# Rows transposed, split and multiplied in two halves of 256 tokens at two of the norms ahead of a projection, and the first loads in another order

## Chip, cores and metric

One core of one Trainium2 chip runs the whole kernel. The metric is the device time of one execution in microseconds (us), the median of three runs. TensorE (PE) multiplies and transposes, VectorE (DVE), ScalarE (ACT) and GpSimd (POOL) work on tiles, and SyncE (SP) issues most of the loads. Each engine works through its own row of instructions, and semaphores hold an instruction back until what it reads is there.

## What is computed

Two transformer blocks over 512 tokens of 1024 channels, in float32. Six times rows are normed and then projected; the change is at the first and the last of the six.

```python
def rms_norm(x, g, eps=NORM_EPS):
    x32 = x.astype(jnp.float32)
    y = x32 * lax.rsqrt(jnp.mean(x32 * x32, axis=-1, keepdims=True) + eps)
    return (y * g.astype(jnp.float32)).astype(x.dtype)

def first_block(x, norm_mix_pre_g, w_in, ...):
    h = rms_norm(x, norm_mix_pre_g[l])
    proj = h @ w_in[l]                       # the first place
    ...
def second_block(x, mem, ...):
    x = x + 0.5 * swiglu(rmsnorm(x, ffn1_norm[l]), ffn1_w_gu[l], ffn1_w_down[l])
    ...
    x = x + memory_cross_attention(rmsnorm(x, mem_q_norm[l]), ..., mem_w_o[l])
    x = x + 0.5 * swiglu(rmsnorm(x, ffn2_norm[l]), ffn2_w_gu[l], ffn2_w_down[l])   # the last place
    return rmsnorm(x, final_norm)
```

## The kernel before

Tokens lie in four tiles of 128 (t), channels in eight tiles of 128 (k). A float32 product is made of three: each operand is split into a high and a low half (`split`, lines 399 to 406: ScalarE writes the high half, VectorE subtracts it from the source for the low half), and high x high, high x low and low x high are added up in a PSUM bank. Weights come in slabs of 1024 rows by 256 columns, a `wr` tile that two DMAs of 512 KB fill; each of its two parts of 128x1024 elements is halved into `wh` and `wl` (lines 402 and 403).

`PreNorm.operand` (line 475) turns normed rows into the right operand of the next projection and multiplies the first slab at once. Its steps, with the names of the trace:

- `scale` (lines 469 to 474): per token tile, two instructions on ScalarE and VectorE scale the rows by their reciprocal root, into `y` tiles of 128x512. At the first place the sums of squares go ahead of it (lines 454 and 563), then a sum (447) and a power on GpSimd (448).
- `flip` (line 489): TensorE transposes, 32 in all. One PSUM bank `b` per k holds 512 tokens. The first six k (`AHEAD`) are transposed token tile by token tile, the last two between the products.
- `split` with the gain (lines 405 and 406): bank k becomes two tiles `h` of 128x512, high and low.
- products (line 513): for each k six of 128x512 columns into the two banks `a`.

TensorE's row is in the order of the program text here (`manual_schedule`). The rows of the other engines are set by a scheduler that goes by priorities: loads and halvings of weights have a high one (`WPRIO`), the splits of the norm too (`SPRIO`), and `in_order` ties the first three splits and one halving of weights (`LATER`, `PINS`) into one order. `later` holds the second halving of the first slab. The next slab is halved among the splits.

`x_rows` (line 188) issues the eight loads of x, each 256 KB. The first place stands at line 569, the last at line 1771, where `wide` (line 1103), the projection ahead of it, multiplies token tile by token tile and its `emit` adds (line 1677), squares and scales each finished tile.

Of the kernel before, what the change touches and what calls it, by code (L numbers as in the profile page):

```python
# [18 lines left out]
P = 128  # L19
# [74 lines left out]
def transformer_blocks_kernel(  # L94
# [55 lines left out]
    def big(tag, bufs, dt=F32, cols=512):  # L150
        return sp.tile([P, cols], dt, tag=tag, bufs=bufs, name=nm(tag))
# [13 lines left out]
    def acc():  # L165
        return pa.tile([P, 512], F32, tag="a", name=nm("a"))

    def aux():
        return pb.tile([P, 512], F32, tag="b", name=nm("b"))
# [15 lines left out]
    junk = cp.tile([P, 512], F32, name="junk")  # L185
    junk2 = sp.tile([P, 512], F32, tag="w", bufs=WBUFS, name="junk2")

    def x_rows(src, get=None):

        res = {}  # L190
        for t in range(4):
            for u in range(2):
                tl = (get or wt)()
                tc.keep_in_program_order(
                    nc.sync.dma_start(tl, src[t * P:(t + 1) * P, u * 512:(u + 1) * 512]))
                res[t, u] = tl
        return res

    with tc.high_priority(2 * WPRIO):
        vec0 = wt()[:8, :P]  # L200
        nc.sync.dma_start(vec0, norm_mix_pre_g.rearrange("a (k p) -> (a k) p", p=P))
        xt = x_rows(x[0])
        gps = aux()
        T.transpose(gps[:, :8], vec0, ident[:8, :8])
        gain0 = cp.tile([P, 8], F32, name="gain0")
        V.tensor_copy(gain0, gps[:, :8])
# [54 lines left out]
    def wload(raw, src, k, n, cols):  # L261
        with tc.high_priority(WPRIO):
            nc.sync.dma_start(raw[:, :n * cols].rearrange("p (k c) -> p k c", c=cols),
                              src[k * P:(k + n) * P, :].rearrange("(k p) c -> p k c", p=P))

    def wslab(src, kt, cols, later=None):
        return list(wpieces(src, kt, cols, later))

    def wpieces(src, kt, cols, later=None):

        per = max(1, 1024 // cols)
        for k in range(0, kt, per):
            n = min(per, kt - k)
            if k % (2 * per) == 0:
                whole = raw_slab()
            raw = whole[:, k % (2 * per) * cols:][:, :n * cols]
            wload(raw, src, k, n, cols)
            hi, lo = [t[:, :n * cols] for t in halves_w()]
            halve = lambda hi=hi, lo=lo, raw=raw: split(hi, lo, raw)
            if later is None or k == 0:  # L280
                with tc.high_priority(WPRIO):
                    halve()
            else:
                later.append(halve)
            yield k, n, hi.rearrange("p (k c) -> p k c", c=cols), lo.rearrange("p (k c) -> p k c", c=cols)
# [128 lines left out]
    @contextmanager  # L414
    def in_order(chain):

        traced = nc.cur_bb.bb.instructions
        last = traced[-1]
        yield
        start = next(k for k in reversed(range(len(traced))) if traced[k] is last) + 1  # L420
        for i in traced[start:]:
            if i.engine in QUEUES:
                if i.engine in chain:
                    tc.add_manual_dep(i, chain[i.engine], mybir.DependencyInfo(
                        mybir.DependencyClass.NoSync, mybir.DependencyReason.DATA))
                chain[i.engine] = i.name
# [30 lines left out]
    class PreNorm:  # L457
# [18 lines left out]
        def operand(self, src, *before):  # L476
# [36 lines left out]
                            T.matmul(accs[m], lh, rh, start=c == 0 and n in (0, 2), stop=c == KT - 1 and n > 3)  # L513
            return res, accs

    class PostNorm:


# [47 lines left out]
                if t:  # L566
                    pre.scale(t - 1, [xt[t - 1, 0], xt[t - 1, 1]], rs[t - 1], act=t < 4)
    with tc.issue_after(pows[-1].ins):
        h, ready = pre.operand(w_in[0][:, :256])

# [1195 lines left out]
        weave(chains, fills, WIDTH3, BANKS3, MODEL3)  # L1768
    pre, emit = residual("ffn2")
    wide(mem_w_o_2[0], KT, mo, emit, WIDE_K, True, begun, HELD)  # L1770
    h, ready = pre.operand(ffn2_w_gu_2[0][:, :256])


    fg = []
# [54 lines left out]
```

## Time and profile before

| | us |
|---|---|
| median of 3 runs (1914.20 to 1915.53) | 1914.49 |
| profiled execution | 1915.45 |
| its span | 1913.7 |
| PE busy (98% of the span) | 1881.5 |
| DVE busy (72%) | 1387.2 |
| ACT busy (49%) | 929.2 |
| POOL busy (9%) | 175.0 |

The share of the chain that ended last is 88% PE. Mean traffic is 101 GB/s, the DMA queue that carries nearly all of it is busy for 29.8% of 16 engines' span. Busy shares are means over stages with different limits, so a place is read by the rows of its own stretch: start and duration in us, then the engine, the line and the tiles (output <- inputs), and in brackets how long the engine had sat idle before and what ended that. "x3" merges three instructions in a row.

### The profile page before, as it was taken

How to read it: one execution, taken by the hardware profiler on the slowest of the kernel's cores; microseconds unless marked ns; L12 is line 12 of the kernel's file. 1: busy time of each engine (PE TensorE's matmuls, PEld its weight loads, DVE VectorE, ACT ScalarE, POOL GpSimd, SP SyncE). 2: the span in 40 equal slices, each digit the busy share in tenths (PEclk: the TensorE clock that was granted, in tenths of full speed). 3: DMA queues.
4: the chain of work that ended last, by engine and by line, in shares of the span. 5: the costliest groups of instructions: out<-in, count | busy, mean ns of one | idle time of the engine just before them, and what ended most of it. 6: DMA issues, size and time to landing. Idle time of an engine off the chain costs nothing.

```text
span 1913.7 us, 29312 instructions
## 1 busy us (share of the span) xinstructions
PE 1881.5 (98%) x11566; PEld 1688.7 (88%) x11566; DVE 1387.2 (72%) x2217; ACT 929.2 (49%) x1537; POOL 175.0 (9%) x272
## 2 busy tenths in 40 slices
PE   8999999999999999999999999999999999999998
PEld 7899888888999998889999988888978778999997
DVE  6777635468878786677878757888866448878785
ACT  5666534364544344444344456668555344344443
POOL 2240100050000002000000010330510000000000
PEclk9999999999999999999999999999989999999999
DMA  5221223462232324423232343211223222332322
GB/s 180 67 67 56 78 66 133 143 203 89 89 111 89 114 97 168 151 89 102 97 111 88 111 148 101 67 45 45 89 89 110 77 81 82 102 111 89 111 89 89
DMA packets 161452, 192.40 MB, mean 101 GB/s; under 512 B 7361, under 2 KB 131362, under 8 KB 161314
## 3 DMA queue, kind: packets, MB, share of 16 engines
q1 hardware_dynamic: 159746, 185.80, 29.8%
q0 software_dynamic: 1280, 4.20, 0.6%
q8 instruction: 91, 1.49, 0.3%
q10 hardware_dynamic: 288, 0.52, 0.1%
q14 instruction: 47, 0.39, 0.1%
HBM read 182.11 MB, written 8.39 MB: 100 GB/s over the span
## 4 chain that ended last, share of the span: by engine, by line
PE 88%; issue 5%; DVE 3%; ACT 2%; POOL 2%; POOLq 0%; ACTq 0%; DVEq 0%
PE b L372 16%; PE b L373 16%; PE b L371 16%; PE a L371 11%; PE a L372 11%; PE a L373 11%; PE a L513 4%; PE b L615 1%; PE b L1444 1%; PE b L489 1%; DVE wl L403 1%; PE b L753 1%; DVE w L1540 0%; ACT wh L402 0%; PE b L883 0%
## 5 line engine op out<-in xcount | busy, mean ns | idle before, releaser
L403 DVE TENSOR_TENSOR wl<-wr,wh 128x1024 fp32r<-128x1024 f32 (+1 forms) x381 | 463.5, 1220 | 269.9 <-ACT wh L402 266.1
L402 ACT CAST wh<-wr 128x1024 fp32r<-128x1024 f32 (+1 forms) x381 | 394.0, 1036 | 443.0 <-PE b L372 154.5
L371 PE MATMUL b<-wh,q 128*128 128x512 f32 x672 | 262.4, 390 | 0.0
L372 PE MATMUL b<-wl,q 128*128 128x512 f32 x672 | 262.0, 390 | 0.0
L373 PE MATMUL b<-wh,q 128*128 128x512 f32 x664 | 257.9, 389 | 0.0
L371 PE MATMUL a<-h,wh 128*128 128x512 f32 (+1 forms) x660 | 238.4, 361 | 0.0
L373 PE MATMUL a<-h,wl 128*128 128x512 f32 (+1 forms) x660 | 234.9, 356 | 0.0
L372 PE MATMUL a<-h,wh 128*128 128x512 f32 (+1 forms) x660 | 234.7, 356 | 0.0
L372 PE MATMUL b<-h,wh 128*128 128x256 f32 (+1 forms) x568 | 175.9, 310 | 0.0
L371 PE MATMUL b<-h,wh 128*128 128x256 f32 (+1 forms) x568 | 175.9, 310 | 0.0
L373 PE MATMUL b<-h,wl 128*128 128x256 f32 (+1 forms) x568 | 175.9, 310 | 0.0
L371 PEld LDWEIGHTS b<-wh,q 128*128 128x128 f32 x672 | 126.3, 188 | 24.7
L373 PEld LDWEIGHTS b<-wh,q 128*128 128x128 f32 x664 | 124.6, 188 | 26.5
L372 PEld LDWEIGHTS b<-wl,q 128*128 128x128 f32 x672 | 126.3, 188 | 24.3
L372 PE MATMUL a<-s,wh 128*128 128x256 f32 (+1 forms) x488 | 141.2, 289 | 0.0
L373 PEld LDWEIGHTS a<-h,wl 128*128 128x128 f32 x660 | 124.5, 189 | 18.3
L371 PEld LDWEIGHTS a<-h,wh 128*128 128x128 f32 x660 | 124.7, 189 | 17.9 <-issue 0.5
L372 PEld LDWEIGHTS a<-h,wh 128*128 128x128 f32 x660 | 124.8, 189 | 17.8 <-issue 0.5
L372 PEld LDWEIGHTS b<-h,wh 128*128 128x128 f32 x568 | 108.3, 191 | 5.6
L373 PEld LDWEIGHTS b<-h,wl 128*128 128x128 f32 x568 | 108.2, 191 | 5.6
L371 PEld LDWEIGHTS b<-h,wh 128*128 128x128 f32 x568 | 108.1, 190 | 5.6
L372 PEld LDWEIGHTS a<-s,wh 128*128 128x128 f32 x488 | 93.1, 191 | 1.3
(374 smaller groups left out, 4195.9 us busy)
## 6 DMA issues: line engine op xcount, KB each, us to landing
wr<-in_ffn_w_gu_dram SPq DMA_DIRECT2D x88, 512.0 KB
wr<-in_w_in_dram SPq DMA_DIRECT2D x68, 512.0 KB
wr<-in_ffn_w_down_dram SPq DMA_DIRECT2D x44, 512.0 KB
wr<-in_w_gate_dram SPq DMA_DIRECT2D x22, 512.0 KB
wr<-in_w_up_dram SPq DMA_DIRECT2D x22, 512.0 KB
wr<-in_w_down_dram SPq DMA_DIRECT2D x22, 512.0 KB
wr<-in_mem_w_kv_dram SPq DMA_DIRECT2D x16, 512.0 KB
wr<-in_w_out_dram SPq DMA_DIRECT2D x10, 512.0 KB
```

Source lines behind the costliest of these rows:

```text
L371: T.matmul(ps, lh, rh, start=first, stop=False)
L372: T.matmul(ps, lh, rl, start=False, stop=False)
L373: T.matmul(ps, ll, rh, start=False, stop=last)
L402: A.copy(hi, src)
L403: V.tensor_tensor(lo, src, f32(hi), op=ALU.subtract)
L489: T.transpose(banks[k][:, t * P:(t + 1) * P], self.s[t, k // 4][:, (k % 4) * P:(k % 4 + 1) * P], ident)
L513: T.matmul(accs[m], lh, rh, start=c == 0 and n in (0, 2), stop=c == KT - 1 and n > 3)
L615: T.matmul(ps, lh[n], rh[n], start=n == 0, stop=n == 1)
L753: T.transpose(ps[:, o * P:(o + 1) * P], blk, ident)
L1444: T.matmul(ps[:, gg * 64:(gg + 1) * 64], e[:, gg * P:(gg + 1) * P], up, start=True, stop=True)
```

## The change

A second method, `operand_by_halves`, is used at the first and at the last norm. A bank now holds two k of 256 tokens. The transposes of tokens 0 to 255 come first, then their splits (128x256) and products (128x256 columns) for six k, then the transposes of tokens 256 to 511, the other two k, and the splits and products of the second half. At the first place the loads go in the order x of tokens 0 to 255, first part of the first weight slab, x of the rest, second part; `wslab` takes that slab as `loaded`.

```diff
@@ -185,10 +185,10 @@
     junk = cp.tile([P, 512], F32, name="junk")
     junk2 = sp.tile([P, 512], F32, tag="w", bufs=WBUFS, name="junk2")
 
-    def x_rows(src, get=None):
+    def x_rows(src, get=None, tokens=range(4)):
 
         res = {}
-        for t in range(4):
+        for t in tokens:
             for u in range(2):
                 tl = (get or wt)()
                 tc.keep_in_program_order(
@@ -199,7 +199,14 @@
     with tc.high_priority(2 * WPRIO):
         vec0 = wt()[:8, :P]
         nc.sync.dma_start(vec0, norm_mix_pre_g.rearrange("a (k p) -> (a k) p", p=P))
-        xt = x_rows(x[0])
+        xt = x_rows(x[0], tokens=range(2))
+        raw0 = sp.tile([P, 2048], F32, tag="wr", bufs=2, name="wr0")
+        for k in (0, 4):
+            tc.keep_in_program_order(
+                nc.sync.dma_start(raw0[:, k * 256:(k + 4) * 256].rearrange("p (k c) -> p k c", c=256),
+                                  w_in[0][k * P:(k + 4) * P, :256].rearrange("(k p) c -> p k c", p=P)))
+            if k == 0:
+                xt.update(x_rows(x[0], tokens=range(2, 4)))
         gps = aux()
         T.transpose(gps[:, :8], vec0, ident[:8, :8])
         gain0 = cp.tile([P, 8], F32, name="gain0")
@@ -263,18 +270,21 @@
             nc.sync.dma_start(raw[:, :n * cols].rearrange("p (k c) -> p k c", c=cols),
                               src[k * P:(k + n) * P, :].rearrange("(k p) c -> p k c", p=P))
 
-    def wslab(src, kt, cols, later=None):
-        return list(wpieces(src, kt, cols, later))
-
-    def wpieces(src, kt, cols, later=None):
+    def wslab(src, kt, cols, later=None, loaded=None):
+        return list(wpieces(src, kt, cols, later, loaded))
+
+    def wpieces(src, kt, cols, later=None, loaded=None):
 
         per = max(1, 1024 // cols)
         for k in range(0, kt, per):
             n = min(per, kt - k)
-            if k % (2 * per) == 0:
+            if loaded is not None:
+                whole = loaded
+            elif k % (2 * per) == 0:
                 whole = raw_slab()
             raw = whole[:, k % (2 * per) * cols:][:, :n * cols]
-            wload(raw, src, k, n, cols)
+            if loaded is None:
+                wload(raw, src, k, n, cols)
             hi, lo = [t[:, :n * cols] for t in halves_w()]
             halve = lambda hi=hi, lo=lo, raw=raw: split(hi, lo, raw)
             if later is None or k == 0:
@@ -513,6 +523,51 @@
                             T.matmul(accs[m], lh, rh, start=c == 0 and n in (0, 2), stop=c == KT - 1 and n > 3)
             return res, accs
 
+        def operand_by_halves(self, src, loaded=None):
+
+            with tc.manual_schedule(engines={mybir.EngineType.PE}):
+                later, chain = [], {}
+                slab = {k + j: (hi[:, j, :], lo[:, j, :]) for (k, n, hi, lo) in wslab(src, KT, 256, later, loaded)
+                        for j in range(n)}
+                accs = [acc() for m in range(2)]
+                res = [(big("h", 16, F32R), big("h", 16, F32R)) for k in range(KT)]
+
+                def flips(half):
+
+                    banks = [aux() for k in range(0, KT, 2)]
+                    for t in range(2):
+                        for k in range(KT):
+                            o = k % 2 * 256 + t * P
+                            T.transpose(banks[k // 2][:, o:o + P],
+                                        self.s[2 * half + t, k // 4][:, (k % 4) * P:(k % 4 + 1) * P], ident)
+                    return banks
+
+                def operands(half, banks):
+                    sl = slice(half * 256, half * 256 + 256)
+                    for k in range(KT):
+                        with tc.high_priority(SPRIO), in_order(chain) if half == 0 and k <= PINS else nullcontext():
+                            split(*[t[:, sl] for t in res[k]], banks[k // 2][:, k % 2 * 256:k % 2 * 256 + 256],
+                                  gcol(self.g, k))
+                            if half == 0 and k == LATER:
+                                later[0]()
+
+                def products(half, ks):
+                    sl = slice(half * 256, half * 256 + 256)
+                    for c in ks:
+                        hh, hl = [t[:, sl] for t in res[c]]
+                        terms = [(slab[c][part][:, m * P:(m + 1) * P], hh, m) for m in range(2) for part in range(2)]
+                        terms += [(slab[c][0][:, m * P:(m + 1) * P], hl, m) for m in range(2)]
+                        for n, (lh, rh, m) in enumerate(terms):
+                            T.matmul(accs[m][:, sl], lh, rh, start=c == 0 and n in (0, 2), stop=c == KT - 1 and n > 3)
+
+                operands(0, flips(0))
+                products(0, range(AHEAD))
+                banks = flips(1)
+                products(0, range(AHEAD, KT))
+                operands(1, banks)
+                products(1, range(KT))
+            return res, accs
+
     class PostNorm:
 
 
@@ -566,7 +621,7 @@
                 if t:
                     pre.scale(t - 1, [xt[t - 1, 0], xt[t - 1, 1]], rs[t - 1], act=t < 4)
     with tc.issue_after(pows[-1].ins):
-        h, ready = pre.operand(w_in[0][:, :256])
+        h, ready = pre.operand_by_halves(w_in[0][:, :256], raw0)
 
 
 
@@ -1768,7 +1823,7 @@
         weave(chains, fills, WIDTH3, BANKS3, MODEL3)
     pre, emit = residual("ffn2")
     wide(mem_w_o_2[0], KT, mo, emit, WIDE_K, True, begun, HELD)
-    h, ready = pre.operand(ffn2_w_gu_2[0][:, :256])
+    h, ready = pre.operand_by_halves(ffn2_w_gu_2[0][:, :256])
 
 
     fg = []
```

ScalarE at the first place, from the load of its table on. In the rows `w` are x tiles (w_82 and w_86 of token tiles 0 and 1), `y` scaled rows, `wr` raw weights, `h` the halves, `b` banks of transposes, `c` sums and powers. Before:

```order
L454 ACTIVATE junk,c_103<-w_82 128x512
L454 ACTIVATE junk,c_111<-w_86 128x512
L471 ACTIVATE y_119<-w_82,c_108 128x512
L454 ACTIVATE junk,c_123<-w_90 128x512
L471 ACTIVATE y_131<-w_86,c_116 128x512
L454 ACTIVATE junk,c_135<-w_94 128x512
L471 ACTIVATE y_143<-w_90,c_128 128x512
L402 CAST wh_155<-wr_153 128x1024
L405 ACTIVATE h_194<-b_164,gain_100 128x512
L405 ACTIVATE h_198<-b_165,gain_100 128x512
```

And after:

```order
L464 ACTIVATE junk,c_106<-w_82 128x512
L412 CAST wh_156<-wr_90 128x1024
L464 ACTIVATE junk,c_114<-w_86 128x512
L481 ACTIVATE y_122<-w_82,c_111 128x512
L464 ACTIVATE junk,c_126<-w_92 128x512
L481 ACTIVATE y_134<-w_86,c_119 128x512
L464 ACTIVATE junk,c_138<-w_96 128x512
L415 ACTIVATE h_164<-b_180,gain_103 128x256
L481 ACTIVATE y_146<-w_92,c_131 128x512
L415 ACTIVATE h_166<-b_180,gain_103 128x256
L415 ACTIVATE h_168<-b_181,gain_103 128x256
L412 CAST wh_160<-wr_90 128x1024
```

The cast of the first weights has moved from behind the scaled rows to a place ahead of the second sum of squares, and one scaling of the second half stands between the first two splits. VectorE's row follows it: the low half of the first weights stands ahead of its sum of squares of token tile 1.

VectorE at the last place, from the scaling of token tile 3 on (the last `y`). Before:

```order
L473 TENSOR_SCALAR y_15721<-w_14665,c_15716 128x512
L406 SCALAR_TENSOR_TENSOR h_15767<-b_15736,gains,h_15766 128x512
L406 SCALAR_TENSOR_TENSOR h_15771<-b_15737,gains,h_15770 128x512
L406 SCALAR_TENSOR_TENSOR h_15775<-b_15738,gains,h_15774 128x512
L403 TENSOR_TENSOR wl_15733<-wr_15725,wh_15732 128x1024
L406 SCALAR_TENSOR_TENSOR h_15781<-b_15739,gains,h_15780 128x512
L403 TENSOR_TENSOR wl_15870<-wr_15867,wh_15869 128x1024
L406 SCALAR_TENSOR_TENSOR h_15785<-b_15740,gains,h_15784 128x512
L406 SCALAR_TENSOR_TENSOR h_15789<-b_15741,gains,h_15788 128x512
```

And after (the splits of half 0 up to k = 5):

```order
L483 TENSOR_SCALAR y_15785<-w_14729,c_15780 128x512
L416 SCALAR_TENSOR_TENSOR h_15801<-b_15816,gains,h_15800 128x256
L416 SCALAR_TENSOR_TENSOR h_15803<-b_15816,gains,h_15802 128x256
L416 SCALAR_TENSOR_TENSOR h_15805<-b_15817,gains,h_15804 128x256
L413 TENSOR_TENSOR wl_15797<-wr_15789,wh_15796 128x1024
L416 SCALAR_TENSOR_TENSOR h_15807<-b_15817,gains,h_15806 128x256
L413 TENSOR_TENSOR wl_15998<-wr_15995,wh_15997 128x1024
L416 SCALAR_TENSOR_TENSOR h_15809<-b_15818,gains,h_15808 128x256
L413 TENSOR_TENSOR wl_16003<-wr_15995,wh_16002 128x1024
L416 SCALAR_TENSOR_TENSOR h_15811<-b_15818,gains,h_15810 128x256
```

The splits keep their places among the halvings of the weights (`wl`), each split has half the columns, and the third halving, which stood behind all eight splits, now stands ahead of the sixth. At both places the eight splits of half 1 follow, even k first. On ScalarE each split of an odd k waits for VectorE, on whose split of the even k in the same bank it depends.

## Rows read from the trace of the kernel before

**Rows 1.** Busy time by stretch: start:end, length, busy per engine, granted clock, DMA.
```profile
0.00:26.50 26.50, 18.15 (x82) 15.01 (x83) 17.12 (x36) 15.95 (x26) 10.43 (x18) 1.00 0.69 224
26.50:395.00 368.50, 368.16 (x2020) 320.53 (x2019) 232.14 (x514) 192.47 (x384) 51.42 (x60) 1.00 0.28 92
1555.00:1573.00 18.00, 16.55 (x86) 13.28 (x86) 11.96 (x17) 12.52 (x18) 1.10 (x2) 1.00 0.31 99
1573.00:1900.00 327.00, 327.00 (x2154) 301.62 (x2154) 257.96 (x345) 133.76 (x179) 0.55 (x1) 1.00 0.30 97
```

**Rows 2.** Chain that ended last, both places: start, length, engine, output, line.
```profile
11.71 2.82 PE b L489 x12
...
18.29 8.21 PE a L513 x36
...
1555.94 0.69 DVE w L1677
...
1560.63 1.65 PE a L513 x6
1562.29 0.44 PE b L489 x4
...
1564.56 8.21 PE a L513 x36
```

**Rows 3.** Timeline of the first place, and the first reading of the gains.
```profile
7.29 0.69 DVE L563 CUSTOM_DVE_ANT_0 junk<-w 128x512 f32<-128x512 f32 x1 [1.37 <-DMA w<-in_x_dram]
...
8.39 0.73 POOL L448 TENSOR_TENSOR c<-c,mhalf 128x1 f32<-128x1 f32 x1 [0.64 <-DVE c L447]
...
9.07 0.69 DVE L563 CUSTOM_DVE_ANT_0 junk<-w 128x512 f32<-128x512 f32 x1 [0.37 <-DMA w<-in_x_dram]
...
11.96 1.05 ACT L402 CAST wh<-wr 128x1024 fp32r<-128x1024 f32 x1 [0.30 <-DMA wr<-in_w_in_dram]
...
13.39 1.16 DVE L403 TENSOR_TENSOR wl<-wr,wh 128x1024 fp32r<-128x1024 f32 x1
...
13.50 1.84 ACT L405 ACTIVATE h<-b,gain 128x512 fp32r<-128x512 f32 x3 [0.50 <-PE b L489]
...
14.24 0.63 PE L513 MATMUL a<-h,wh 128*128 128x512 f32 x1
14.47 2.05 DVE L406 SCALAR_TENSOR_TENSOR h<-b,gain,h 128x512 fp32r<-128x512 f32 x3
...
51.50 0.28 DVE L235 COPY gains<-b 128x128 f32<-128x128 f32 x1
```

**Rows 4.** Timeline of the last place: scaling of token tiles 2 and 3.
```profile
1557.48 0.72 ACT L471 ACTIVATE y<-w,c 128x512 f32<-128x512 f32 x1
...
1558.76 0.48 DVE L473 TENSOR_SCALAR y<-w,c 128x512 f32<-128x512 f32 x1 [0.66 <-POOL c L448]
```

**Rows 5.** Timeline of the norm of `mem`: splits of 128x256.
```profile
329.40 0.48 DVE L406 SCALAR_TENSOR_TENSOR s<-b,gains,s 128x256 fp32r<-128x256 f32 x1
329.80 0.68 DVE L406 SCALAR_TENSOR_TENSOR q<-q,q 128x512 fp32r<-128x512 f32 x1
...
330.58 0.48 ACT L405 ACTIVATE s<-b,gains 128x256 fp32r<-128x256 f32 x1 [0.19 <-PE b L1022]
331.09 0.48 DVE L406 SCALAR_TENSOR_TENSOR s<-b,gains,s 128x256 fp32r<-128x256 f32 x1 [0.18 <-ACT s L405]
331.61 0.47 ACT L405 ACTIVATE s<-b,gains 128x256 fp32r<-128x256 f32 x1 [0.55 <-DVE s L406]
```

**Rows 6.** Chain that ended last: one product of 256 columns.
```profile
1700.08 0.12 PE b L371
```

**Rows 7.** Busy time by stretch, around a wait of PE.
```profile
1390.00:1395.00 5.00, 2.38 (x14) 1.95 (x12) 3.59 (x11) 3.70 (x9) 3.00 (x7) 0.85 0.30 111
1395.00:1400.00 5.00, 5.00 (x19) 3.97 (x19) 3.02 (x9) 2.01 (x5) 0.00 (x0) 0.50 0.00 0
...
1405.00:1410.00 5.00, 5.00 (x36) 4.42 (x35) 3.49 (x11) 3.61 (x10) 0.00 (x0) 1.00 0.01 3
```

## The prediction

> **What bounds the kernel now.** I read the busy time of the engines by stretch first. TensorE (PE) is busy for all but 0.34 us between 26.5 and 395 us and for all 327 us from 1573 to 1900 [rows 1]: what ends later ahead of these stretches makes them end later, and nothing there takes it back. At the two places of the change it is idle: 8.35 us of the first 26.5, and 1.45 us of the 18 from 1555 to 1573. The chain that ended last [rows 2] then shows what is between. At the first place (A) the transposes start last at 11.71 and from 18.29 the products of k = 2 to 7 run as one block of 8.21 us, to 26.50. At the last place (B) the previous projection ends at 1555.92 with the add of token tile 3, the first product starts at 1560.63, and the same block of 8.21 us ends at 1572.77. So before, from the first product on, TensorE hardly waits: a product of 512 columns takes 0.227 us (8.21 / 36), 1.36 us per k, and that covers the splits (ScalarE's activation gives the high half, VectorE's subtraction the low half), with the halvings of weights that stand between them. What the change can win is the wait ahead of the first product.
>
> **Part by part, TensorE.** 48 products of 512 columns at 0.227 = 10.9 us become 96 of 256 at 0.12 [rows 6] = 11.5 us: +0.6 us per place. The 32 transposes stay. But now one k of a half covers only 6 x 0.12 = 0.72 us of split time, where it covered 1.36.
>
> **ScalarE and VectorE.** 8 pairs of splits of 512 columns become 16 of 256. Three ScalarE splits took 1.84 us and three VectorE splits 2.05 [rows 3], 0.74 us for one VectorE split with its successor overlapped to 0.66. A pair of 256 columns takes 0.47 and 0.48 us [rows 5], so two halves cost VectorE about 0.96 us in place of 0.74, or 0.80 in place of 0.66 start to start (329.40 to 329.80). A second price is in the same rows. The new bank of 512 columns holds two k of one half. Banks of that form stand at the norm of `mem`, and there the second ScalarE split of a bank, at 331.61, waited 0.55 us for VectorE's split of the first, although both only read the bank. So the two engines take turns: 1.03 us from one ScalarE split to the next inside a bank.
>
> [...]
>
> **The order.** Each engine takes its instructions in the order shown above, and this decides. In front of the first half's splits stand the same halvings of the weights as before, of both slabs: the slab in use and the next one, which no product of this place needs. A halving costs 1.05 us on ScalarE and 1.16 on VectorE [rows 3]. On VectorE three of them stand before the low half of k = 5, and the transposes of half 1 stand on TensorE behind the products of k = 5. So TensorE starves in half 0 and has more than half of its work left when half 0 is split.
>
> **Place B, walked along that order** with the start-to-start steps of the rows (split 0.40, halving about 1.0 on ScalarE and 1.1 on VectorE, 13.39 to 14.47, a few hundredths from engine to engine). ScalarE reaches the first split only behind the scaling of token tile 2 (1557.48 to 1558.2, [rows 4]), so at 1558.2; VectorE reaches its low half only behind the scaling of tile 3, issued beside ScalarE's at 1558.76 for 0.48 us, so at 1559.24. Then: high half of k = 1 at 1559.75 (it waits for VectorE), low half 1560.25; halving of the slab's second part; low half of k = 3 at 1562.7; halving; k = 4 at 1564.2; halving; k = 5 at 1565.75. TensorE ends k = 5 at 1566.5. Behind it stand 16 transposes at 0.11 to 0.12 [rows 2], 12 products of k = 6 and 7, 48 of half 1: 1.87 + 1.44 + 5.76 = 9.07 us. End 1575.56. The same walk along the order of before ends at 1572.40, where the trace has 1572.77. **+3.2 us.**
>
> **Place A.** The loads: the weights take the place of two x tiles in the queue, so their first half should land where the sixth x tile did, when VectorE's wait for it ended: 9.07 [rows 3], not 11.96. But ScalarE's cast of it now stands ahead of the square of token tile 1, which landed before 7.29; and VectorE's low half of the weights stands ahead of its square of that tile. Both wait for the load, and the scaling of tile 0 waits with them. Cast 9.07 to 10.1, square of tile 1 to 10.7, scaling of tile 0 at 10.7; on VectorE the low half to 11.3, square and sum of tile 1 to 12.2, then 0.7 us for the power on GpSimd, as at 8.39 [rows 3]; scaling of tile 1 at 13.0 and 13.6; first split 14.3, its low half 15.0. The first product, at 14.24 before, is no earlier, and only half as wide. Then the casts again: second part of the slab at 16.2, next slab at 17.2 and 19.3 or so, low halves k = 3 at 20.0 and k = 5 at 22.5. TensorE starts the transposes of half 1 at 23.25, and 9.07 us later it is done: 32.3. The walk of before gives 26.26, the trace 26.50. **+5.8 us** (32.3 - 26.5). GpSimd now does its constants ahead of the four powers, at nothing, since the first power waits for loads and sums; without that cover the one that is under way would delay it, by about 1 us. On SyncE the next weights are issued ahead of most loads of gains; those are first read at 51.50 [rows 3], by my estimate some 20 us after they can land, and if that were short TensorE would show it as idle time after 26.5. Elsewhere the order is unchanged. The slab's buffers stay in use until half 1 is multiplied, some 7 us longer; the next cast in them then has about 10 us before its product, behind 48 products of the next slab.
>
> **TensorE's clock, a cost without a row here.** [...] The half-0 stretch at B would be busy 4.3 (36 x 0.12) of some 8 us. [...] Bounds: 0, and at each place the 1.87 + 1.44 us behind k = 5 doubled, +3.3. No gain is possible. I take +1.0 in all, near the low end, since no gap in half 0 is longer than about 1.1 us while the fall stands in a stretch with 2.62 us idle.
> [...]
>
> **Sum.** The profiled execution took 1915.45 us, 1.75 more than its span. 1915.45 + 5.8 + 3.2 + 1.0 = 1925.45; it lies 0.96 above the median of 1914.49, so **1924.5 us**.
>
> **Rivals.**
> - **C, the clock falls at both places** for the tail behind k = 5: +9.0 + 6.6, 1930.1; at one place 1926.8. For it: [rows 7]. [...]
> - **L, the first weights do not come earlier.** The load of rows of 1 KB may end only with the x tiles behind it, at 11.96: everything at A is 2.9 us later, 1926.4 without the clock's term. The opposite, a landing at 7.3, takes 1.8 off: 1921.7.
> - **O, the other side: half 0 does cover the wait.** If the splits keep ahead of the products from the first one on, place B ends with TensorE's own work: 1555.92 + 32 x 0.117 + 96 x 0.12 = 1571.2, -1.6; at A the products start where the transposes of the first six k did, at 11.71 [rows 2], and end 96 x 0.12 + 16 x 0.117 = 13.4 us later, at 25.1, -1.4. That is 1911.5. It decides from the point at which VectorE has the low half of k = 5 ready within 4.3 us of the first split, 1562.5 at B; the three halvings ahead of it speak against that.
> - **H, hidden.** Both places lose as walked, and stages that wait later give it back: within 2 us of before. Against it: 0.34 us of idle in 368 [rows 1].
>
> **Chances.** Forecast, +7 to +11.5: 0.58; C 0.17; L, either way, 0.13; O 0.07; H 0.05. Likeliest is the forecast. The range leaves out O, H and the end of C: 1918 to 1930. A measurement of this kernel tells 0.2%, 3.8 us, from no change. O's 3.0 us is inside that, so faster needs O and more: 0.03; same 0.09; slower 0.88.
>
> **What would show it.** In the changed trace: ScalarE's first weight cast at about 9 waiting for its load, and the scaling of tile 0 behind it near 10.7; the first product of A at about 14.3; gaps of TensorE ahead of products, released by VectorE's split, with the last of them at k = 5; turns of about 1.03 us between the two engines' splits of one bank; end of A near 32 and of B some 3 us later, counted from the add of tile 3. It would be wrong if products of half 0 at B follow without gaps, or if the stretch behind A has idle time that it had not before.

## The result and the profile after

The changed kernel takes 1926.61 us (median of five runs, 1923.27 to 1928.99) against 1915.45 (median of five, 1914.20 to 1915.98): a ratio of 1.0059, 95% interval [1.0048, 1.0070]. It is slower, by 11 us or 0.6%, and the predicted 1924.5 with its range of 1918 to 1930 holds it. The profiled execution took 1925.06 us with a span of 1923.4, 9.7 us more than the span of before.

Busy time by stretch of the kernel after, cut where [rows 1] was cut; the columns are start and end, length, busy time of PE, PEld, DVE, ACT and POOL, granted clock, DMA share, GB/s (the stretch of the last place is left out):

```profile
0.00:33.38 33.38, 19.56 (x130) 17.97 (x131) 18.89 (x44) 17.15 (x34) 9.42 (x18) 1.00 0.60 194
33.38:401.88 368.50, 368.16 (x2019) 320.52 (x2018) 231.95 (x514) 192.36 (x384) 51.35 (x60) 1.00 0.28 91
1582.50:1909.50 327.00, 327.00 (x2154) 301.62 (x2153) 257.65 (x345) 133.57 (x179) 0.55 (x1) 1.00 0.29 95
```

The second and the third row are those of before: 368.16 us busy of 368.5, and 327.00 of 327. Nothing behind either place gives time back. TensorE's wait in the first stretch grew from 8.35 to 13.82 us.

The chain that ended last, first at the first place (A), then at the last (B); start, length, engine, output, line:

```profile
3.08 6.21 DMA wr<-in_w_in_dram
...
9.32 1.05 ACT wh L412
...
10.40 1.23 DVE wl L413
...
13.39 0.73 ACT y L481
...
19.52 1.42 DVE wl L413
20.93 0.39 DVE h L416
...
26.18 7.20 PE a L561 x60
...
1562.68 0.69 DVE w L1732
...
1572.49 0.41 DVE h L416
...
1573.45 1.75 PE b L541 x16
1575.19 7.19 PE a L561 x60
```

At A the chain now begins with the load of the first weights, goes through the cast of them and VectorE's low half of them to the scaling of token tile 1, and further on through low halves of weights again. Before, it was TensorE's own work from 11.71 on [rows 2]. A ends at 33.38 (26.18 + 7.20 for the last 60 products), 6.88 us later than before. B ends at 1582.38, 19.70 us behind the start of the add of token tile 3, where before it was 16.83 (1564.56 + 8.21 - 1555.94): 2.87 us more. Together 9.75, which is the 9.7 of the spans.

The timeline of A, as [rows 3] for before:

```profile
9.32 1.04 ACT L412 CAST wh<-wr 128x1024 fp32r<-128x1024 f32 x1 [4.42 <-DMA wr<-in_w_in_dram]
...
10.90 0.71 ACT L481 ACTIVATE y<-w,c 128x512 f32<-128x512 f32 x1
...
13.00 3.13 PE L541 MATMUL b<-ident,y 128*128 128x128 f32 x12 [0.23 <-DVE y L483]
...
15.79 0.56 PE L561 MATMUL a<-h,wh 128*128 128x256 f32 x1
...
18.26 2.67 DVE L413 TENSOR_TENSOR wl<-wr,wh 128x1024 fp32r<-128x1024 f32 x2
...
21.38 0.62 PE L561 MATMUL a<-h,wh 128*128 128x256 f32 x3 [1.57 <-DVE h L416]
...
22.91 0.89 PE L561 MATMUL a<-h,wh 128*128 128x256 f32 x3 [0.55 <-DVE h L416]
```

And before, the scaling of tile 0:

```profile
7.31 0.70 ACT L471 ACTIVATE y<-w,c 128x512 f32<-128x512 f32 x1
```

ScalarE waits 4.42 us for the load with its cast, with the scaling of tile 0 (10.90) queued behind. TensorE's waits of 1.57 and 0.55 us are released by VectorE's splits. At B its longest waits in half 0 are 0.97, 0.33 and 0.28 us (at 1565.36, 1566.43 and 1572.94). They look short because the products themselves went at about half pace for a part of half 0 (0.21 us from one start to the next between 1568.13 and 1570.9, 0.12 between 1567.16 and 1567.5; granted clock 0.50 from 1568 to 1571); the chain there goes through VectorE.

### The profile page after: what moved, and what is told of

The parts are those of the page before. It is cut to its first block, busy times and chain, and to the rows that moved or that the text cites. A ratio compares the mean times of both kernels' runs of the same rounds, so it can differ in the third digit from the quotient of the medians.

```text
span 1923.4 us, 29544 instructions
## 1 busy us (share of the span) xinstructions
PE 1885.8 (98%) x11662; PEld 1696.2 (88%) x11662; DVE 1389.3 (72%) x2233; ACT 931.5 (48%) x1553; POOL 173.9 (9%) x272
## 4 chain that ended last, share of the span: by engine, by line
PE 86%; DVE 5%; issue 5%; ACT 2%; POOL 1%; DMA 0%; SPq 0%; POOLq 0%; DVEq 0%; ACTq 0%
PE b L382 16%; PE b L383 15%; PE b L381 15%; PE a L381 10%; PE a L382 10%; PE a L383 10%; PE a L523 2%; DVE wl L413 1%; PE b L670 1%; PE b L1499 1%; PE a L561 1%; DVE w L1595 1%; PE b L808 1%; ACT wh L412 1%; PE b L499 1%
```

## The experiments

**Theories.** Mine: TensorE starves in half 0 because of the order in which ScalarE and VectorE take their instructions; each place costs by itself. The rivals: the load order alone, the turns in one bank of PSUM, the granted clock, and the halves as such. The measure is the end of a place in the trace, since one execution differs from the next elsewhere (last section): for A the end of the first slab's products, for B the time from the start of the add of tile 3 to the end of the slab's products. From B's end to the end of the span it is 340.9 to 341.0 us in every run, so no variant loses or wins anything later. Each end is that of one profiled execution.

```
run                   ratio to before, 95%      end of A   B from the add
before                                           26.50      16.83
after                 1.0059 [1.0048, 1.0070]    33.38      19.70
after_again           1.0053 [1.0039, 1.0067]    34.48      19.70
a_only                1.0027 [1.0017, 1.0037]    34.18      16.82
b_only                1.0015 [1.0006, 1.0023]    26.29      19.71
a_halves_old_loads    1.0020 [1.0011, 1.0029]    29.94      16.83
a_loads_only          1.0013 [1.0004, 1.0022]    30.11      16.82
a_cast_late           1.0017 [1.0008, 1.0026]    31.12      16.83
b_banks               1.0013 [1.0004, 1.0022]    26.36      19.41
b_hold                1.0012 [1.0003, 1.0020]    27.27      18.67
b_hold_busy           1.0006 [0.9998, 1.0015]    27.34      18.08
b_early               0.9996 [0.9987, 1.0005]    26.83      see there
b_early_again         0.9995 [0.9986, 1.0003]    26.95      see there
```

Where A is as before, its end still lies between 26.29 and 27.34: an end of A is good to about half a microsecond. B's figure repeats to 0.01 us wherever B is the same.

### One place at a time

a_only and b_only are the changed kernel with one place put back (cut to the lines that matter, as all edits below are):

```diff
 a_only:
-    h, ready = pre.operand_by_halves(ffn2_w_gu_2[0][:, :256])
+    h, ready = pre.operand(ffn2_w_gu_2[0][:, :256])
 b_only (and x_rows as before, in one call):
-        h, ready = pre.operand_by_halves(w_in[0][:, :256], raw0)
+        h, ready = pre.operand(w_in[0][:, :256])
```

> The first place in halves with the loads in the new order, the second place as before. My theory (the two places cost apart from each other, by the order of ScalarE and VectorE inside each): the first slab's products end at 33.4 us as in the trace of after, against 26.50 before, and nothing else moves: +6.9 us, ratio 1.0036. Rival, the clock: part of the 9.7 us belongs to TensorE's clock over the whole run and appears only with both places changed; then this run and the one that changes only the second place add up to clearly less than 9.7. Rival, one place hides the other: this run alone has all of the 9.7, or none.

> The second place in halves, the first norm and its loads as before. My theory: from the start of the add of token tile 3 to the end of the slab's products 19.7 us against 16.8 before, all else as before: +2.9 us, ratio 1.0015. Rival, the clock: the stretch of half-0 products at the lower level (0.66 to 0.77 of full speed in the trace of after) costs more than the 2.9, so that this run is slower than that, and its runs lie further apart than those of before (1.8 us between the lowest and the highest there, 5.7 in after).

The places are apart from each other: each trace has its own place as in after (a_only's A 0.8 us later) and the other as in before. By the times a_only is 5.2 us slower [3.3, 7.1] and b_only 2.9 [1.1, 4.4], where their places lost 7.7 and 2.9. The two ratios add up to 8.0 us, below the 9.7 and 11.2 of after but not outside the intervals. The eleven times of b_only lie within 4.2 us, those of before from the same session within 4.4, so the wider runs that the clock rival asked for are not there. The missing part of a_only lies between the places, in its profiled execution: 1526.74 us from A's end to the add, against 1529.44 before.

The same kernel as after, a second time:

> The changed kernel once more, as it is, to see which of its stretches differ between two executions. Theory: the first place ends at 33.4 to 34.2 (33.38 in after, 34.18 in the run with the first place alone), the second takes 19.7 from the add to the end of the products, the stretch from there to the end 341.0 as in every run, and the stretch between the places varies by up to 3.3 us (1529.4 before, 1526.2 in the run with halves and old loads) by how long the clock stands at 0.50 near 1400: a span of 1920 to 1924 and a ratio of 1.004 to 1.006. Rival, the 9.7 us are real to the tenth and the stretch between varies by the change: ratio 1.005 or more and the runs no wider than those of before.

Span 1921.9, ratio 1.0053, runs from 1921.66 to 1926.63: as expected, though the 34.48 of A is over the range named. The ratio alone would fit the rival too; what speaks for the theory is that the same kernel needed 1526.8 us between the places here and 1529.3 in after. What differs at A is the clock. Busy time of the 2 us from 24, in after_again, then in after (columns as above):

```profile
24.00:26.00 2.00, 2.00 (x12) 2.00 (x11) 0.48 (x1) 0.30 (x1) 0.00 (x0) 0.50 1.08 359
```
```profile
24.00:26.00 2.00, 2.00 (x21) 2.00 (x19) 0.76 (x2) 0.91 (x3) 0.00 (x0) 1.00 1.08 349
```

TensorE is busy throughout in both, with 12 instructions at 0.50 and 21 at 1.00. The 16 transposes of half 1 took 3.03 us in after_again (in the chain), 2.94 in a_only, 1.75 in after. From the start of these transposes in the chain to the end of A it is 8.94 us in after, 10.21 in after_again and 10.13 in a_only. So the rival C of the prediction did happen at A, in two of three profiled executions, for 1.2 to 1.3 us and not for 3.3.

### What the first place is made of

> The first place in halves, but the loads in the old order (all rows of x first, then the weights), the second place as before. ScalarE then has its three scalings ahead of its first cast, and that cast waits for the weights until about 11.96 as before. My theory, by the same walk of the queues: splits of half 0 start at 11.4 instead of 14.9, first product near 14.8, the casts of both slabs stand among the half-0 splits and each odd k waits for VectorE, VectorE's last half-0 split near 21.2, the slab's products end at 29.6 to 30.2, against 26.50 before and 33.38 after: +3.1 to +3.7 us, 1918.9, ratio 1.0018. Rival, the loads are the whole cost at this place: the end is at 26.5 and the time is that of before. Rival, the halves are the whole cost and the loads nothing: end at 33.4, +6.9.

```diff
-        xt = x_rows(x[0], tokens=range(2))
-        raw0 = ...            # and the two early loads of weights
+        xt = x_rows(x[0])
-        h, ready = pre.operand_by_halves(w_in[0][:, :256], raw0)
+        h, ready = pre.operand_by_halves(w_in[0][:, :256])
```

The second place is as before. From TensorE's timeline one row, then its chain at A:

```profile
15.06 0.58 PE L554 MATMUL a<-h,wl 128*128 128x256 f32 x1 [1.73 <-DVE wl L406]
```
```profile
15.06 5.94 PE a L554 x35
...
22.75 7.19 PE a L554 x60
```

End 29.94, as walked (29.6 to 30.2), so the halves without the loads cost 3.4 us. The way there is not the one walked. The first product starts at 12.94, not at 14.8, and TensorE then waits 1.73 us for VectorE's low half of the first weights. From 15.06 on it has no gap, because its products start 0.21 us apart up to 18.4 (granted clock 0.50 from 16 to 18). It was close: VectorE began the low half of k = 5 at 19.93 and had it about 20.4, and TensorE took it up at 20.60. So the order of VectorE's work alone would have held the end at 29.7, and the clock added at most 0.2 us.

> Only the new load order at the first place (the first slab's weights between the second and the third token tile of x, with ScalarE's cast and VectorE's subtraction of them as early in their queues as in after); the operand in one piece of 512 tokens, the second place as before. My theory: the cast waits for the weights until 9.3 and holds the square of tile 1 and the scaling of tile 0 behind it (scaling of tile 0 at 10.9, against 7.3 before), VectorE's last scaling ends near 17.0 against 13.4, first product near 17.6 to 18.1 against 14.24, then no starvation: products end at 29.4 to 29.9: +2.9 to +3.4 us, 1918.6, ratio 1.0017. Rival, the loads are the whole cost of the first place: +6.9. Rival, they are hidden: the early weights save the wait for them and the end is at or before 26.5, time as before or lower.

```diff
-        def operand(self, src, *before):
+        def operand(self, src, *before, loaded=None):     # handed on to wslab
-        h, ready = pre.operand_by_halves(w_in[0][:, :256], raw0)
+        h, ready = pre.operand(w_in[0][:, :256], loaded=raw0)
```

The second place is as before here too. The chain at A:

```profile
9.50 1.05 ACT wh L412
...
17.98 1.66 PE a L523 x6
...
21.90 8.21 PE a L523 x36
```

First product at 17.98 (14.24 before), then the same block of 8.21 us as before without a gap, end 30.11, a little over the walk's 29.9. Here the load order by itself costs 3.6 us, and all of it ahead of the first product. Both rivals, that one of the two parts is the whole cost, are out: 3.4 and 3.6 add up to 7.0, against 6.88 to 7.98 for both.

> Only the first place in halves with the loads in the new order, but ScalarE's cast of the first weights and VectorE's subtraction queued behind the scaling of tile 1 (they land behind ScalarE's scaling of tile 2 and VectorE's of tile 3). My theory, the early cast holds up the scalings: scaling of tile 0 back at 7.3 as before, first product near 16.0, the products end at 30.7 instead of 33.38 to 34.18: +4.2 us against before instead of the +6.9 to +7.7 by the trace. What is left is the later landing of tiles 2 and 3 and the halves. Rival, the cast's place is nothing and the later rows of x are all: end at 33 or more, +6.9.

```diff
     halve = lambda ...: split(hi, lo, raw)
+    # first piece of the loaded weights: behind the scaling of tile 1
+    with tc.issue_after(pre.scaled[1, 0]), tc.issue_after(pre.scaled[1, 1]):
+        split(hi, lo, raw)
```

The edit is told here in short form; the second place is as before. Timeline: on ScalarE the scaling of tile 0 and the cast, then TensorE's second product.

```profile
6.65 0.71 ACT L486 ACTIVATE y<-w,c 128x512 f32<-128x512 f32 x1
...
13.24 1.03 ACT L417 CAST wh<-wr 128x1024 fp32r<-128x1024 f32 x1
...
16.26 0.58 PE L566 MATMUL a<-h,wl 128*128 128x256 f32 x1 [1.36 <-DVE wl L418]
```

The scaling of tile 0 is at 6.65, even ahead of the 7.31 of before, and A ends at 31.12 (23.92 and 7.20 in the chain), 2.3 us before after and 3.4 before after_again, with the loads in the new order. So the place of the cast was worth two to three of the seven microseconds. First product 14.32, earlier than the 16.0 that I had walked; what was gained there was lost again in half 0, first in the 1.36 us for the low half of the weights. The end is 0.4 us behind the 30.7 of the walk.

### What the last place is made of

> Only the second place in halves, and there k and k+4 share a bank of PSUM instead of k and k+1, so that ScalarE's split of k=1 no longer stands behind VectorE's of k=0; the halvings of the own and the next slab stay among the half-0 splits. Measured from the add of token tile 3 to the end of the slab's products: 16.83 before, 19.71 with the second place in halves. My walk gives 0.3 us less than 19.71, 19.4, since VectorE's subtractions of both slabs (3 x 1.13) fill the time in which the turns were waited for: +2.6 us against before. Rival, the turns of 1.03 us are the main cause of the starvation: 17.7 or less, +0.9 or less.

```diff
-    T.transpose(banks[k // 2][:, o:o + P], ...      # o = k % 2 * 256 + t * P
+    T.transpose(banks[k % 4][:, o:o + P], ...       # o = k // 4 * 256 + t * P; the splits read there
```

The chain, from the add:

```profile
1555.88 0.69 DVE w L1725
...
1564.26 1.13 DVE wl L406
1565.39 0.41 DVE h L409
...
1568.09 7.20 PE a L554 x60
```

19.41 against 19.71: the turns are worth 0.3 us here. With them gone VectorE's subtractions of weights still stand in the chain, the last of them right ahead of the low half that TensorE waits for. At A the turns were not taken out by themselves: in after ScalarE's split of k = 5 began at 22.89, having waited 2.56 us for VectorE's of k = 4 in the same bank, so their price there stays open.

> Only the second place in halves, and the next slab's two casts and two subtractions queued behind the splits of half 1 instead of among those of half 0 (the turns in one bank stay). My theory, the engine order: VectorE's last half-0 split comes 9.5 us after the add instead of 11.2, products of half 1 begin at 12.2 instead of 13.8, and from the add to the end of the products 18.0 instead of 19.71: +1.2 us against before instead of +2.9, nothing lost later since the next slab's products start 3 us or more behind its halvings. Rival, the turns in one bank are the cause: 19.4 to 19.7, no change against the second place alone. Rival, the next slab then comes late: 18.0 for this slab and a gap of up to 1.6 us ahead of the next.

```diff
-    halve = lambda hi=hi, lo=lo, raw=raw: split(hi, lo, raw)
+    # the next slab's two pieces: behind the last split of half 1, on either engine
+    with tc.issue_after(last[0].ins), tc.issue_after(last[1].ins):
+        split(hi, lo, raw)
```

(In short form: the kernel carries the two splits over in a list.) The chain, from the add:

```profile
1556.87 0.69 DVE w L1736
...
1561.13 5.47 PE a L564 x30
...
1568.35 7.19 PE a L564 x60
```

18.67: 1.04 us better, not the 1.7 of the walk. The chain says where the rest is: from 1560.62 to the end it is TensorE alone, and 30 products take 5.47 us, 0.18 each in place of 0.12. The clock in that stretch:

```profile
1562.00:1565.00 3.00, 3.00 (x16) 2.94 (x15) 2.04 (x4) 1.66 (x5) 0.00 (x0) 0.50 0.07 10
```

At 0.50 TensorE was busy all the time (3.00 of 3.00 us) and its own products set the pace. To tell the clock from my walk's error:

> Only the second place in halves, the next slab's halvings behind the splits of half 1, and eleven transposes of the identity into a bank that nobody reads, in TensorE's two waits there: eight behind the transposes of half 0, three ahead of k=0's products with the second term. They are added work. In the run without them this place took 18.67 us from the add to the end of the products where my walk gave 18.0, with a granted clock of 0.50 from about 5 us to 8.5 us behind the add, after waits of 1.2 and 0.4 us. Theory: the fall follows those waits, so with TensorE kept at work the clock stays at 1.00 and the place takes 18.0 us. Rival, the fall comes with the products themselves: 0.50 again and 18.7. Rival, the eleven transposes cost their 0.117 us each, 1.3 us: 19.3 to 20.

```diff
     operands(0, flips(0))
+    busy(8)                    # T.transpose(idle[:, :P], ident, ident), eight times
     products(0, range(AHEAD))  # and busy(3) in k = 0 ahead of the terms with the low half
```

Its added transposes (timeline of PE), the chain behind them, and the clock where it had been 0.50:

```profile
1555.83 1.04 PE L559 MATMUL b<-ident 128*128 128x128 f32 x8
...
1557.54 0.49 PE L559 MATMUL b<-ident 128*128 128x128 f32 x3
```
```profile
1561.50 1.94 PE a L570 x14
...
1565.18 7.19 PE a L570 x60
```
```profile
1559.00:1562.00 3.00, 2.45 (x19) 2.10 (x18) 2.41 (x5) 1.66 (x4) 0.00 (x0) 1.00 0.02 5
```

The add is at 1554.29, the end at 1572.37: 18.08, as walked, with added work in the queue. So in one execution the clock fell to 0.50 behind TensorE's waits (0.97 and 0.33 us in the timeline of b_hold, not 1.2 and 0.4), and in one it stayed at 1.00 with most of them filled. That the added transposes kept it up is not shown: in b_banks, with waits of 0.97, 0.33 and three of about 0.55 us that nothing filled, it read 1.00 from 1557 to 1568, and the times of b_hold and b_hold_busy (1.0012 and 1.0006) have intervals that overlap. The place took 0.6 us less at 1.00 than at 0.50 in these two traces.

The 18.08 is still 1.25 us above the 16.83 of before. By the products' own times 0.6 us of it are the pieces of 256 columns (96 x 0.12 against 48 x 0.227); the rest, with the turns still in it, was not taken apart.

### Half 0 ahead of the products that it had to wait for

> Only the second place in halves; the 16 transposes of half 0 stand in TensorE's queue in the middle of the products of token tile 3 of the block ahead (tiles 0 and 1 are scaled by then), its splits behind them, the next slab's halvings behind the splits of half 1. My theory, a half pays only where its splits are done before TensorE is free: the add of tile 3 comes 1.9 us later (16 transposes ahead of it), the products of half 0 then start at once (k=0 to 2 are split by then) and TensorE goes through 192 products and 16 transposes with gaps of 0.2 us in all: from the add to the end of the products 13.5 us, with the 1.9 ahead of it 15.4 against 16.83 before: -1.4 us, ratio 0.9993. Rival, the halves themselves cost (the 0.64 us of products in pieces of 256 columns, the splits in pieces): no less than before. Rival, the splits of half 0 hold up the add and the scaling of tiles 2 and 3: gap ahead of half 1, time as before or more.

(Its "192 products" is a slip of mine: it is 96 products and 16 transposes, and the 13.5 us are worked out from these.)

```diff
     for n_, p_ in enumerate(slab):
         piece(t, *p_)
+        if t == 3 and n_ == 1 and midway is not None:
+            midway()           # transposes and splits of half 0
...
-    wide(mem_w_o_2[0], KT, mo, emit, WIDE_K, True, begun, HELD)
-    h, ready = pre.operand_by_halves(ffn2_w_gu_2[0][:, :256])
+    with tc.manual_schedule(engines={mybir.EngineType.PE}):
+        wide(mem_w_o_2[0], KT, mo, emit, WIDE_K, True, begun, HELD, pre.first_half)
+        h, ready = pre.second_half(ffn2_w_gu_2[0][:, :256])
```

The next slab's halvings are held back as in b_hold. One thing more is different: the slab's own second halving is no longer tied in among the splits of half 0, and VectorE takes both low halves of these weights in a row at 1553.04, ahead of its first split. Timeline: VectorE's add of token tile 2, and TensorE, then the end of the chain.

```profile
1549.81 0.69 DVE L1737 TENSOR_TENSOR w<-w,b 128x512 f32<-128x512 f32 x1 [3.48 <-PE b L385]
...
1552.33 1.91 PE L534 MATMUL b<-ident,y 128*128 128x128 f32 x16
...
1561.30 0.51 PE L564 MATMUL a<-h,wh 128*128 128x256 f32 x2 [0.24 <-DVE h L418]
```
```profile
1563.55 7.20 PE a L564 x60
```

And before, the add of token tile 2:

```profile
1550.50 0.69 DVE L1677 TENSOR_TENSOR w<-w,b 128x512 f32<-128x512 f32 x1 [3.48 <-PE b L373]
```

Since the transposes now stand ahead of the add of tile 3, I count from the add of tile 2. The slab's products end at 1570.75 (1563.55 + 7.20), 20.94 us behind it; before it is 22.27 (1572.77 - 1550.50). That is -1.33 us where -1.4 was expected. The products of half 0 start at 1556.83, and TensorE waits once, 0.24 us. By the times the two measurements give 0.9996 and 0.9995 with intervals that reach over 1:

> The second place with half 0 ahead of the last products, as it ran, once more for a closer interval: 20.9 us from the add of tile 2 to the end of the products against 22.27 before (-1.33 in the first trace), so a ratio of 0.9993. Rival, no gain: 1.0000.

The second trace has 20.93 us again. So a half does cover the wait once its splits, and the halvings that stood among them, are done ahead of it, and b_early beats the changed kernel clearly. That it beats the kernel before is shown in the trace by 1.3 us, and not by the time.

## Why the prediction was right

**The sum.** The parts were 5.8 + 3.2 + 1.0 = 10.0 us, and the spans differ by 9.7. That they agree so closely is partly luck: place A was 1.1 too small, place B 0.3 too large, and the clock's 1.0 is not found at the two tails of the profiled execution. The median is 11.2 us above the 1915.45 measured with it, but 12.1 above the 1914.49 that the prediction started from, which is past the +7 to +11.5 of its forecast and within its range.

**The bound.** Right: idle time behind both places is unchanged (368.16 us busy of 368.5 behind A, 327.00 of 327 behind B), and what the places lost came through whole.

**TensorE's products and the split prices.** 0.12 us per product of 256 columns held (7.20 / 60). The splits took 0.47 and 0.48, and the turns are there: at B ScalarE's split of k = 1 waits 0.19 us for VectorE's of k = 0 (1566.41), that of k = 5 0.60 us for VectorE's of k = 4 (1571.40). ScalarE's first two splits at A start 1.03 us apart (14.89 and 15.92), but a scaling of 0.71 us stands between them.

**Place B, +3.2.** It was 2.87. The walk of after put the low half of k = 5 9.81 us behind the add, and VectorE began it 9.73 behind (1572.41 in its timeline; the chain counts it from 1572.49, where the halving ahead of it ends); its end was 0.1 short (19.6). What was off is the walk of before, 16.46 against 16.83, which I had subtracted. Of the reasons named, the next slab's halvings weigh most (1.0 us, 1.6 in the execution in which the clock stayed up). The turns in a bank, which I gave as the "second price", weigh 0.3. Some 1.25 us were left with the next slab's halvings out of half 0 and the clock up, of which 0.6 are the products in pieces that the prediction had named.

**Place A, +5.8.** It was 6.88 in after and 7.7 to 8.0 in two other executions. The mechanism was right in both its parts, each shown alone (3.4 and 3.6), the halves by another way than I had walked for that run. The size was short by 1.1 in after, in four terms of the walk: the load landed at 9.3, not 9.07 (0.25); the first split came at 14.89, not 14.3 (another 0.34: the scaling of tile 1 at 13.39 was 0.14 later than the load explains, and behind it 0.2 more went by at the transposes of half 0, which took 0.26 us each, 3.13 / 12); VectorE's two low halves of weights took 2.67 us where I had 1.1 for each (0.3 by the low half of k = 3, at 20.85, not 20.0); and 0.2 up to the transposes of half 1 (24.28, not 23.25). The first product came at 15.79, not 14.3: I had named the time of the first split as its time, and left out that TensorE's own transposes of half 0 stand ahead of it. The last wait of half 0 that a split released was at k = 4 (22.91), and not at k = 5 as I had named it; at B it was at k = 5.

**The clock, +1.0.** No run shows this term as it stands in the sum: it was my choice between bounds. In the profiled execution the clock cost nothing at the two tails, where it read 1.00. It did fall in half 0 at B, but only where the splits set the pace anyway:

```profile
1568.00:1571.00 3.00, 3.00 (x16) 3.00 (x16) 2.79 (x4) 2.80 (x5) 0.00 (x0) 0.50 0.15 15
```

At A it took 1.2 to 1.3 us in two other executions, at 0.50 from 24 to 26. I had the term near the low end for the reason that no gap in half 0 would be longer than 1.1 us, against the fall to 0.50 behind 2.62 us of idle time in [rows 7]. That did not hold: at B the clock fell to 0.50 behind gaps of 0.97 and 0.33 us, while at A it stayed at 1.00 behind 1.57 and 0.55 in after and fell to 0.50 behind 1.39 and 0.55 in a_only. So the size of 1.0 was near what two executions showed at A, but the reason given for it was wrong. What decides whether the clock falls behind a wait is not shown: behind 0.97 and 0.33 us it went to 0.50 in b_hold and stayed at 1.00 in b_banks.

**The rivals.** L is out: the early weights landed at 9.3. H is out: the stretches behind A and B are as busy as before. C happened at A in part of the executions (0.50 from 24 to 26 in after_again and a_only, 1.00 in after). O did not happen, for the reason given: VectorE began the low half of k = 5 9.73 us behind the add, and O needed it 6.6 behind (1562.5 - 1555.94). b_early gives the other side of the same rule: with the splits early, the gain that O promised at B, -1.6, comes to -1.33.

## What to carry to other kernels

Cutting an operand in two helped here only where the first part's splits were finished before TensorE was free; otherwise the smaller pieces halved the work that hides each split (six products of a k: 0.72 us in place of 1.36), and the weight halvings among them in the queues showed. Look at what stands ahead in ScalarE's and VectorE's queues before moving a load forward: here a load issued early brought the cast and the subtraction that wait for it ahead of scalings which were ready. Where TensorE must wait, find out what the clock does behind the wait, because a part of the gain of a shorter wait was lost there in b_hold (30 products at 0.18 us each in place of 0.12, with the granted clock at 0.50 from 1562 to 1565).

## What was not expected of the hardware

**The stretch between the places differs by 3 us from one execution to the next, with the same instructions.** From A's end to the add of tile 3 it took 1529.4 us before, 1529.3 in after, 1526.8 in after_again and 1526.1 in a_halves_old_loads. The place is a wait near 1390 [rows 7]. The same kernel twice, after and then after_again:

```profile
1400.00:1405.00 5.00, 4.51 (x16) 3.51 (x16) 3.68 (x12) 2.83 (x7) 0.00 (x0) 0.54 0.00 0
1405.00:1410.00 5.00, 5.00 (x20) 4.71 (x21) 2.87 (x5) 1.24 (x2) 0.00 (x0) 0.50 0.01 3
```
```profile
1400.00:1405.00 5.00, 3.50 (x14) 2.50 (x15) 4.69 (x15) 3.61 (x8) 0.62 (x2) 0.73 0.01 2
1405.00:1410.00 5.00, 5.00 (x38) 4.87 (x38) 3.26 (x7) 2.14 (x6) 0.00 (x0) 0.93 0.01 3
```

Busy throughout from 1405 to 1410 in both, TensorE did 20 instructions in one and 38 in the other; TensorE's wait was the same (17.38 us busy of the 20 from 1395 in both), the stretch at 0.50 behind it was not (a mean of 0.54 and 0.50 in the two rows of after, 0.73 and 0.93 in those of after_again). That is as much as most effects of this study, so single times could not have told them apart; the ends of the places in the trace could.

**A place with added work ended sooner.** With eleven transposes that nobody reads, B took 18.08 us in place of 18.67, in one execution each; that they were the reason is not shown.

**The clock's column does not tell all.** In the first 18 us of A it reads 1.00 while products of 256 columns start 0.21 us apart, and later 0.12. The trace of after holds clock records only from 17.99 us on (14.54 before), just where the pace changes; ahead of them the 1.00 stands for no record (timeline of PE, after):

```profile
16.15 0.41 PE L561 MATMUL a<-h,wl 128*128 128x256 f32 x1
16.36 0.41 PE L561 MATMUL a<-h,wh 128*128 128x256 f32 x1
...
18.40 0.28 PE L561 MATMUL a<-h,wl 128*128 128x256 f32 x1
18.52 0.28 PE L561 MATMUL a<-h,wh 128*128 128x256 f32 x1
```

Whether VectorE's slower subtractions at A (2.67 us for two, 1.34 each, against 1.16 for the first in [rows 3]) come from GpSimd, which was busy for 1.88 of the 2 us from 18 there, was not tried; in before, around that 1.16, it was busy for 3.78 of the 4 us from 12.
